# Conformer convolution: tap diagonals on ScalarE in place of GpSimd, lasting padded buffers, the last bias on VectorE

## The chip, the cores and the metric

The kernel runs on one core of a Trainium2 chip. The metric is device time in microseconds (us) of one execution, compared by the median of several runs. The engines are TensorE (PE in the profile: matmuls, with weight loads as PEld), VectorE (DVE), ScalarE (ACT) and GpSimd (POOL); SyncE (SP) issues the DMAs.

## The reference, cut to what matters

Eight residual stages run over 256 tokens of 1024 channels: a state-space and gated linear attention mixer, a feed-forward stage, latent attention, a feed-forward stage, retention with pooling, a feed-forward stage, the conformer convolution, a feed-forward stage. Only the seventh is touched:

```python
def conformer_conv(h, w_pw1, b_pw1, w_dw, b_dw, ln_g, ln_b, w_pw2, b_pw2):
    a, gate = jnp.split(h @ w_pw1 + b_pw1, 2, axis=-1)
    u = a * jax.nn.sigmoid(gate)
    dw = lax.conv_general_dilated(
        u, w_dw[:, None, :], window_strides=(1,), padding=((CONV_WIDTH_2 - 1, 0),),
        dimension_numbers=('NWC', 'WIO', 'NWC'), feature_group_count=D_MODEL) + b_dw
    ...
    z = (d32 - mu) * lax.rsqrt(var + EPS) * ln_g + ln_b
    z = jax.nn.silu(z).astype(h.dtype)
    return z @ w_pw2 + b_pw2
```

The depthwise convolution has 31 taps over time for each of 1024 channels, padded with 30 zeros on the left. The result, with the bias `b_pw2`, is added to the residual x.

## The kernel before

Every float32 product is made in three passes over two halves of each operand. The high half is a ScalarE copy, the low half a VectorE subtraction: for weights `hi` (L151) and `lo` (L152), pieces of 128x512; for activations in `split` (L156, L157). The three matmuls of a product are L283 to L285 (tokens on the output's partitions) or L289 to L291 (channels on them).

The conformer holds channels on partitions, eight channel tiles k of 128 channels. The string `ORDER = "p0 c01 p1 c23 s0 p2 c45 s1 p3 c67 s2 s3"` gives the order in which its steps are written:

- `p0` to `p3`: projection i makes channel tiles 2i and 2i+1. For each there are 48 matmuls of 128x256 into a bank `acc` (p0 has tokens on the partitions, is copied out as `rt`, L1081, and turned), then `sg` = sigmoid (ScalarE, L1096), `u` = gated product (VectorE, L1099), and its halves `uh` (ScalarE) and `ul` (VectorE), 128x286 with the margin of 30 zeros, which a GpSimd memset writes (L1098).
- `c01` to `c67`: the convolution of two channel tiles. `PE_TAPS = [13]*6 + [16, 18]`, 112 in all, says how many of a tile's 31 taps run on TensorE, as matmuls with diagonal matrices into a bank `pw`: three matmuls and two diagonals (high, low) for each tap. `diags` (L1038) makes up to eight taps' diagonals with one GpSimd instruction (L1044), in four rotating buffers `diag`. The other 136 taps are VectorE instructions over `u` that add into `d` (8 at L1141, 128 at L1143); then one instruction per tile adds the bank `pw` to `d` (L1146, the d add below).
- `s0` to `s3`: statistics of d. After `s3`, layer norm, silu (ScalarE, L1186) and the output projection, which adds to x.

The bias bp is added to x by two GpSimd instructions of 128x1024 (L1065) at the stage's start. A scheduler places instructions on each engine's queue by dependencies and priorities (`high_priority`, `issue_after`); each engine then runs its queue in order.

Of the kernel before, what the change touches and what calls it, by code (L numbers as in the profile page):

```python
# [17 lines left out]
P = 128  # L18
# [12 lines left out]
# how far a stage's splits of the weights may go ahead, and in how many steps  # L31
TUNE = [(150, 4), (1, 4), (400, 4), (1, 4), (1, 4), (1, 4), (400, 4), (1, 4)]
FIRST = 800  # priority of the chains that the tensor engine waits for
ORDER = "p0 c01 p1 c23 s0 p2 c45 s1 p3 c67 s2 s3"  # conformer: projections, convolutions, statistics
MORDER = "s0 p0 s1 v0 p1 n1 v1 s2 s3 v2 v3"  # attention: scores, second half of the projections, its norms, values
# [7 lines left out]
def T(t):  # L43
    return slice(t * P, (t + 1) * P)


def bc_row(v, n):
    """a DRAM vector of n values, the same for each partition"""
    return v.rearrange("(o c) -> o c", o=1).to_broadcast([P, n])


def cols(v):
    """a DRAM vector of 128*k values -> [128, k], value k*128+p on partition p"""
    return v.rearrange("(k p) -> p k", p=P)


class Net:
# [32 lines left out]
    def constants_later(self):  # L90
        nc, c, a = self.nc, self.cst, self.a
        g = nc.gpsimd
        self.identb = c.tile([P, P], BF16, name="identb")
        g.tensor_copy(self.identb, self.ident)
        self.tri = c.tile([P, P], F32, name="tri")
        g.affine_select(self.tri, self.ones, pattern=[[1, P]], base=0, channel_multiplier=-1, compare_op=ALU.is_ge, fill=0.0)
        zer = self.tmp.tile([P, 512], F32, tag="sq512", name="zer", bufs=1)
        g.memset(zer, 0.0)
        # SSD: [s, (chunk, l)], masked where l < s
        self.mneg_s = c.tile([P, 2, P], BF16, name="mneg_s")  # L100
        g.affine_select(self.mneg_s, zer[:, :256].rearrange("p (a b) -> p a b", a=2), pattern=[[0, 2], [1, P]], base=0, channel_multiplier=-1, compare_op=ALU.is_ge, fill=NEG)
        # attention: [q, k] masked where k > q
        self.mneg_a = c.tile([P, P], BF16, name="mneg_a")
        g.affine_select(self.mneg_a, zer[:, :P], pattern=[[-1, P]], base=0, channel_multiplier=1, compare_op=ALU.is_ge, fill=NEG)
        # one-hot rows: a head's high part lies in row h, its low part in row 32 + h
        self.sel = c.tile([P, 16], F32R, name="sel")
        self.nc.vector.tensor_add(self.sel, self.ident[:, 0:16], self.ident[:, 32:48])
# [6 lines left out]
    def columns(self, srcs, name, t=None, eng=None):  # L114
        """rows of 128 values in DRAM -> columns, in tiles of up to 128 of them; the second step is returned"""
        nc = self.nc
        n = sum(s.shape[0] for s in srcs)
        assert n <= P
        raw = self.tmp.tile([P, P], F32, tag="raw_col", name="raw_col", bufs=3)
        o = 0  # L120
        for s in srcs:
            (eng or nc.gpsimd).dma_start(out=raw[o:o + s.shape[0], :], in_=s)
            o += s.shape[0]
        if t is None:
            t = self.cst.tile([P, n], F32, name=name)

        def turn():
            b = self.bank("ptr", (P, P))
            nc.tensor.transpose(b[:, :n], raw[:n, :], self.ident[:n, :n])
            nc.vector.tensor_copy(t, b[:, :n])  # L130
        return t, turn

# [27 lines left out]
    def small_weights(self, W):  # L160
        """the columns of dt (0:16) and of the gate's low rank part (32:48)"""
# [9 lines left out]
    def load_x(self, x, g):  # L171
        """-> the first stage's gain on all partitions, in two banks"""
# [34 lines left out]
    def rsqrt_wide(self, v, n, pool):  # L207
        """v [P, n] -> 1 / sqrt(v) in place: a first value from the exponent's bits, three Newton steps"""
# [12 lines left out]
    def transposes(self, src, hi, lo, ncols):  # L221
        """src [128 tokens, ncols] -> hi/lo [128, ncols/128, 128]"""
# [8 lines left out]
    def transposes_f32(self, srcs, dst, rows=P, scale=None, eng="act"):  # L231
        """srcs [128, rows] each -> dst [rows, len, 128]"""
# [60 lines left out]
    def projA(self, w, evac, n=512, tok=(0, 1)):  # L293
        """w [1024, n<=512]: evac(t, bank [128 tokens, n])"""
# [10 lines left out]
    def projW(self, w, evac):  # L305
        """w [1024, 256]: evac(j, psum [128 columns, 256 tokens]) for its two column tiles"""
# [9 lines left out]
    def outproj(self, w, lhs, ks, after, tail=2, ahead=None, pieces=None):  # L316
        """x[t] += lhs^T @ w; after(t) is called when x[t] is whole. ks: order of the k tiles"""
# [72 lines left out]
    def mixer0(self, after):  # L390
# [3 lines left out]
        with self.stage("mix") as sp, self.stage("mixs") as ss:  # L394
# [34 lines left out]
            # ---- gates: log sigmoid, sums within the chunks of 64  # L429
# [14 lines left out]
            # ---- dt = softplus(x) = max(x, 0) + log1p(exp(-|x|)), log1p(e) = 2 atanh(e / (2 + e))  # L444
# [27 lines left out]
            # ---- the gates' sums and their exponentials  # L472
# [10 lines left out]
            # ---- x, B, C: projection, causal convolution, silu  # L483
# [20 lines left out]
            # exponents' parts on partitions: -acum of each chunk, and what is left of chunk 0  # L504
# [16 lines left out]
            # decay0[s, h, l] for s in chunk 0 and all l, decay1 for s and l in chunk 1  # L521
# [23 lines left out]
            # ---- the state-space part, y[p, l] for two heads at a time  # L545
# [8 lines left out]
            # ---- GLA values  # L554
# [3 lines left out]
            # ---- keys and queries with their decays  # L558
# [23 lines left out]
            # ---- GLA. Scores within a token tile: from an even chunk to the odd one the decay of the even chunk comes in  # L582
# [83 lines left out]
    def mla(self, after):  # L666
# [3 lines left out]
        with self.stage("mla") as sp, self.stage("mlap") as pp:  # L670
# [6 lines left out]
            with self.tc.issue_after(self.last_norm):  # L677
# [9 lines left out]
                # the norms' gains over the nope part, both for q  # L687
# [4 lines left out]
            # the low rank projections  # L692
# [5 lines left out]
            for t in range(2):  # L698
# [6 lines left out]
                with self.tc.high_priority(offset=FIRST):  # L705
# [12 lines left out]
                    if t == 1:  # L718
                        # the softmax's table, while the engine is free
                        nc.scalar.activation(ssq[:, 0:1], ssq[:, 0:1], AF.Exp)  # L720
                    nc.vector.tensor_scalar(kr[t].rearrange("p o j -> p (o j)"), c[:, QR + KR:672], r[:, 2:3], None, op0=ALU.mult)
            # rotation with the gains in it: out = x * rc + swap(x) * rs
# [13 lines left out]
            def rope(x, t, i, n):  # L736
                """x [P, n, 32] in SBUF, in place"""
# [11 lines left out]
            # q, k, v by heads, eight at a time  # L749
# [41 lines left out]
            def norms(i):  # L791
# [6 lines left out]
                # q's rope part takes the ratio of its two norms, the rest comes in with the softmax's scale  # L798
# [15 lines left out]
            # attention, four heads at a time  # L814
# [71 lines left out]
    def rotations(self, sp):  # L886
        """sines and cosines of positions * inv_freq: the angle is reduced in two steps with an exact three part 2 pi"""
# [29 lines left out]
        # cos = sin(pi/2 - |r|)  # L917
# [8 lines left out]
    def retention(self, after):  # L926
        nc, a = self.nc, self.a
        W = a["ret_w_in_2"][0]
        with self.stage("ret") as sp, self.stage("retp") as pp:
# [43 lines left out]
            # retention: keys of chunk 0 meet all queries, keys of chunk 1 the queries of theirs  # L973
# [39 lines left out]
            # pooling: sums over windows by doubling  # L1013
# [24 lines left out]
    def diags(self, pool, taps, k):  # L1038
        """the two halves of some taps' weights on diagonals: [128, (tap, half), 128]"""
        n = 2 * len(taps)  # L1040
        t = pool.tile([P, 16, P], F32R, tag="diag", name="diag", bufs=4)
        w = self.whl_dw[:, taps[0] % 2, taps[0] // 2:taps[0] // 2 + len(taps), :, k].rearrange("p a b -> p (a b)")
        w = w.rearrange("p (a o) -> p a o", o=1).to_broadcast([P, n, P])
        self.nc.gpsimd.affine_select(t[:, :n], w, pattern=[[0, n], [1, P]], base=0, channel_multiplier=-1, compare_op=ALU.is_equal, fill=0.0)  # L1044
        return t

    def conformer(self, after):
# [3 lines left out]
        with self.stage("conf") as sp, self.stage("confp") as pp:  # L1051
# [4 lines left out]
            # even taps, then odd ones  # L1056
# [4 lines left out]
            with self.tc.issue_after(self.last_norm):  # L1061
                bp = pp.tile([P, D], F32, name="bp")
                nc.sync.dma_start(out=bp, in_=bc_row(a["conv_b_pw2_2"][0], D))
                for t in range(2):
                    nc.gpsimd.tensor_add(self.x[t], self.x[t], bp)  # L1065
# [3 lines left out]
            def proj(i):  # L1069
                cs = slice(i * 256, i * 256 + 256)  # L1070
                ag = [self.load([W[:, cs]], 8, 256), self.load([W[:, D + i * 256:D + (i + 1) * 256]], 8, 256)]
                if i == 0:
                    # tokens on partitions, so that the first half can start before the second is normed; turned afterwards
# [9 lines left out]
                for j in range(2):  # L1083
# [10 lines left out]
                    with self.tc.high_priority(offset=FIRST):  # L1094
                        sg = sp.tile([P, 256], F32, tag="sg", name="sg", bufs=2)
                        nc.scalar.activation(sg, ps[:, 1, :], AF.Sigmoid, bias=self.bp1[:, 8 + k:9 + k])  # L1096
                        u = sp.tile([P, H + S], F32, tag="u", name="u", bufs=4)
                        nc.gpsimd.memset(u[:, :H], 0.0)  # L1098
# [4 lines left out]
                        if k == 7:  # L1103
                            # the table of the norm's silu, while the engine is free
# [3 lines left out]
            def conv(ks):  # L1108
                """some taps on the tensor engine, the others on the vector engine"""
                bs, rest = {}, {}  # L1110
                for k in ks:
# [5 lines left out]
                    if n_odd:  # L1117
                        # float32r operands start on 8 bytes: a copy that is one ahead for the odd taps
# [45 lines left out]
            # layer norm over the channels: statistics with tokens on the partitions, then mean and deviation along the tokens  # L1164
# [14 lines left out]
            for w in (1, 1, 2, 2, 2):  # L1179
# [8 lines left out]
                k += w  # L1188
            self.outproj(a["conv_w_pw2_2"][0], lambda k, t: (zTh[:, k, T(t)], zTl[:, k, T(t)]), list(range(8)), after, ahead=1)
# [99 lines left out]
```

## Time and profile before

| | us |
|---|---|
| median of 3 runs | 1350.18 |
| lowest, highest | 1350.11, 1351.87 |
| span of the profiled execution | 1351.1 |

The profiled execution has no time beside its span. The span lies within the three runs, so nothing measurable lies around it, and it is 0.9 us above their median. TensorE's mean granted clock is 0.986 of full speed. The conformer's convolutions take 1009.3 to 1119.0 us of the span. The profile is read from the page's totals to the windows of that stretch, then to the waits in it, and to single instructions on the timelines.

### The profile page before, as it was taken

How to read it: one execution, taken by the hardware profiler on the slowest of the kernel's cores; microseconds unless marked ns; L12 is line 12 of the kernel's file. 1: busy time of each engine (PE TensorE's matmuls, PEld its weight loads, DVE VectorE, ACT ScalarE, POOL GpSimd, SP SyncE). 2: the span in 40 equal slices, each digit the busy share in tenths (PEclk: the TensorE clock that was granted, in tenths of full speed). 3: DMA queues.
4: the chain of work that ended last, by engine and by line, in shares of the span. 5: the costliest groups of instructions: out<-in, count | busy, mean ns of one | idle time of the engine just before them, and what ended most of it. 6: DMA issues, size and time to landing. Idle time of an engine off the chain costs nothing.

```text
span 1351.1 us, 21552 instructions
## 1 busy us (share of the span) xinstructions
PE 1289.8 (95%) x8562; PEld 1174.5 (87%) x8562; DVE 874.6 (65%) x1720; ACT 661.4 (49%) x1410; POOL 97.9 (7%) x111
## 2 busy tenths in 40 slices
PE   5999999999999999999999999999999797999997
PEld 4979888999988867999987889999879796999986
DVE  4868565655545887755547777555469997655544
ACT  3783454545544876554444535554443223544542
POOL 3000000000000000000000000000016440000000
PEclk9999999999999999999999999999999897999999
DMA  6546344655554423655655544555653104455551
GB/s 186 168 156 203 116 156 165 203 182 178 179 208 133 162 95 107 226 179 179 213 191 172 184 159 166 177 181 180 217 171 110 68 28 134 164 186 187 187 199 50
DMA packets 152495, 219.75 MB, mean 163 GB/s; under 512 B 8371, under 2 KB 121499, under 8 KB 152396
## 3 DMA queue, kind: packets, MB, share of 16 engines
q1 hardware_dynamic: 151018, 214.04, 47.4%
q0 software_dynamic: 1376, 4.34, 0.9%
q8 instruction: 67, 1.10, 0.3%
q14 instruction: 32, 0.26, 0.1%
q10 hardware_dynamic: 2, 0.00, 0.0%
HBM read 217.33 MB, written 1.05 MB: 162 GB/s over the span
## 4 chain that ended last, share of the span: by engine, by line
PE 81%; DVE 10%; ACT 3%; issue 3%; DMA 1%; POOL 1%; SPq 0%; POOLq 0%; DVEq 0%; ACTq 0%
PE acc L290 11%; PE acc L291 11%; PE acc L289 11%; PE acc L329 8%; PE acc L330 8%; PE acc L333 8%; PE acc L285 4%; PE acc L283 4%; PE acc L284 4%; DVE lo L152 3%; PE pw L289 3%; PE pw L290 3%; PE pw L291 3%; DVE d L1143 2%; PE ptr L228 1%
## 5 line engine op out<-in xcount | busy, mean ns | idle before, releaser
L152 DVE TENSOR_TENSOR lo<-raw,hi 128x512 fp32r<-128x512 f32 (+2 forms) x800 | 515.0, 689 | 239.3 <-ACT hi L151 238.0
L151 ACT CAST hi<-raw 128x512 fp32r<-128x512 f32 (+2 forms) x800 | 444.8, 616 | 312.0 <-PE acc L333 104.2
L291 PE MATMUL acc<-xTh,lo 128*128 128x256 f32 x1312 | 372.7, 284 | 0.7 <-DVE lo L152 0.7
L289 PE MATMUL acc<-xTh,hi 128*128 128x256 f32 x1312 | 373.3, 285 | 0.0
L290 PE MATMUL acc<-xTl,hi 128*128 128x256 f32 x1312 | 372.9, 284 | 0.0
L291 PEld LDWEIGHTS acc<-xTh,lo 128*128 128x128 f32 x1312 | 253.0, 193 | 0.9 <-DVE lo L152 0.9
L290 PEld LDWEIGHTS acc<-xTl,hi 128*128 128x128 f32 x1312 | 253.1, 193 | 0.2
L289 PEld LDWEIGHTS acc<-xTh,hi 128*128 128x128 f32 x1312 | 253.0, 193 | 0.2
L330 PE MATMUL acc<-lo,hTh 128*128 128x512 f32 x352 | 137.3, 390 | 0.0
L329 PE MATMUL acc<-hi,hTh 128*128 128x512 f32 x352 | 137.3, 390 | 0.0
L283 PE MATMUL acc<-hi,xTh 128*128 128x512 f32 (+2 forms) x352 | 120.2, 341 | 0.0
L285 PE MATMUL acc<-hi,xTl 128*128 128x512 f32 (+2 forms) x352 | 119.3, 339 | 0.5 <-DVE xTl L157 0.5
L284 PE MATMUL acc<-lo,xTh 128*128 128x512 f32 (+2 forms) x352 | 119.6, 340 | 0.0
L333 PE MATMUL acc<-hi,hTl 128*128 128x512 f32 x352 | 113.5, 389 | 0.0
L204 POOL TENSOR_TENSOR r<-v,nhalf 128x1 f32<-128x1 f32 (+1 forms) x24 | 16.3, 679 | 993.6 <-DVE v L265 937.3
L289 PE MATMUL pw<-xTh,hi 128*128 128x256 f32 x264 | 76.1, 288 | 8.4 <-ACT xTh L156 8.4
L382 DVE TENSOR_TENSOR h<-sg,acc 128x256 f32<-128x256 f32 x72 | 30.0, 417 | 80.0 <-ACT sg L381 79.8
L381 ACT ACTIVATE sg<-acc 128x256 f32<-128x256 f32 x72 | 27.6, 383 | 104.8 <-PE acc L291 98.8
L333 PEld LDWEIGHTS acc<-hi,hTl 128*128 128x128 f32 x352 | 66.1, 188 | 13.6
L329 PEld LDWEIGHTS acc<-hi,hTh 128*128 128x128 f32 x352 | 66.1, 188 | 13.6
L330 PEld LDWEIGHTS acc<-lo,hTh 128*128 128x128 f32 x352 | 66.1, 188 | 13.4
L290 PE MATMUL pw<-xTl,hi 128*128 128x256 f32 x264 | 76.1, 288 | 0.0
(399 smaller groups left out, 1889.9 us busy)
## 6 DMA issues: line engine op xcount, KB each, us to landing
raw<-w_in_even SPq DMA_DIRECT2D x22, 1024.0 KB, 5.1
raw<-w_gate SPq DMA_DIRECT2D x22, 1024.0 KB, 5.3
raw<-w_up SPq DMA_DIRECT2D x22, 1024.0 KB, 5.3
raw<-w_down SPq DMA_DIRECT2D x22, 1024.0 KB, 4.8
raw<-ffn_w_gate SPq DMA_DIRECT2D x22, 1024.0 KB, 5.2
raw<-ffn_w_up SPq DMA_DIRECT2D x22, 1024.0 KB, 5.1
raw<-ffn_w_down SPq DMA_DIRECT2D x22, 1024.0 KB, 4.8
raw<-conv_w_pw SPq DMA_DIRECT2D x12, 1024.0 KB, 5.2
```

What stands on the lines that cost most here:

```text
L151: nc.scalar.copy(fl(hi)[:, c], fl(raw)[:, c])
L152: nc.vector.tensor_sub(fl(lo)[:, c], fl(raw)[:, c], f32(fl(hi)[:, c]))
L283: mm(out, lh, wh, start=first, stop=False)
L284: mm(out, lh, wl, start=False, stop=False)
L285: mm(out, ll, wh, start=False, stop=last)
L289: mm(out, wh, xh, start=first, stop=False)
L290: mm(out, wh, xl, start=False, stop=False)
L291: mm(out, wl, xh, start=False, stop=last)
L329: nc.tensor.matmul(b, lh, hi[:, j, cs], start=st, stop=False)
L330: nc.tensor.matmul(b, lh, lo[:, j, cs], start=False, stop=False)
L333: nc.tensor.matmul(banks[t][h], ll, hi[:, j, cs], start=False, stop=sp)
L382: nc.vector.tensor_mul(h, sg, ps[:, 1, :])
```

## The change

`diags` fills the same four rotating buffers, but by 224 ScalarE instructions of 128x128, each a copy of the identity scaled by one column of `whl_dw` (a scale that is read from memory, one value per partition). The GpSimd instruction is gone. The tiles `u` are four lasting buffers, whose margins are cleared once at the stage's start (four memsets instead of eight). The bias is added to x on VectorE, and stands in the code just ahead of the output projection. In other functions comments alone are removed.

```diff
     def diags(self, pool, taps, k):
-        n = 2 * len(taps)
         t = pool.tile([P, 16, P], F32R, tag="diag", name="diag", bufs=4)
-        w = self.whl_dw[:, taps[0] % 2, taps[0] // 2:taps[0] // 2 + len(taps), :, k].rearrange("p a b -> p (a b)")
-        w = w.rearrange("p (a o) -> p a o", o=1).to_broadcast([P, n, P])
-        self.nc.gpsimd.affine_select(t[:, :n], w, pattern=[[0, n], [1, P]], base=0, channel_multiplier=-1, compare_op=ALU.is_equal, fill=0.0)
+        for n, tap in enumerate(taps):
+            for half in range(2):
+                w = f32(self.whl_dw[:, tap % 2, tap // 2, half, k:k + 1])
+                self.nc.scalar.activation(t[:, 2 * n + half, :], self.ident, AF.Copy, scale=w)
         return t
...
                 nc.sync.dma_start(out=bp, in_=bc_row(a["conv_b_pw2_2"][0], D))
-                for t in range(2):
-                    nc.gpsimd.tensor_add(self.x[t], self.x[t], bp)
+
+                ubuf = [sp.tile([P, H + S], F32, name=f"u{i}") for i in range(4)]
+                for u in ubuf:
+                    nc.gpsimd.memset(u[:, :H], 0.0)
...
-                        u = sp.tile([P, H + S], F32, tag="u", name="u", bufs=4)
-                        nc.gpsimd.memset(u[:, :H], 0.0)
+                        u = ubuf[k % 4]
...
+            for t in range(2):
+                nc.vector.tensor_add(self.x[t], self.x[t], bp)
             self.outproj(a["conv_w_pw2_2"][0], lambda k, t: (zTh[:, k, T(t)], zTl[:, k, T(t)]), list(range(8)), after, ahead=1)
```

The scheduler also moves instructions that the diff doesn't name. The rows below are instructions in queue order: line, operation, output and inputs, the output's shape, and a count where a row repeats.

On VectorE, at the end of `p0`, from the split of the convolution's weights (`whl_dw`) to the first low halves `ul`, the queue of before is:

```order
L157 TENSOR_TENSOR whl_dw<-wdw,whl_dw 128x15x8
L152 TENSOR_TENSOR lo<-raw,hi 128x512 x8
L1099 SCALAR_TENSOR_TENSOR u<-acc,lp,sg 128x256 x2
L1141 TENSOR_SCALAR d<-u,wdw,lp 128x256
L157 TENSOR_TENSOR ul<-u,uh 128x286 x2
```

and the queue of the change at the same place is:

```order
L157 TENSOR_TENSOR whl_dw<-wdw,whl_dw 128x15x8
L1191 TENSOR_TENSOR x_82<-x_82,bp 128x1024
L1191 TENSOR_TENSOR x_83<-x_83,bp 128x1024
L152 TENSOR_TENSOR lo<-raw,hi 128x512 x5
L1100 SCALAR_TENSOR_TENSOR u_10214<-acc,lp,sg 128x256
L1100 SCALAR_TENSOR_TENSOR u_10215<-acc,lp,sg 128x256
L152 TENSOR_TENSOR lo<-raw,hi 128x512
L157 TENSOR_TENSOR ul<-u_10214,uh 128x286
L157 TENSOR_TENSOR ul<-u_10215,uh 128x286
L152 TENSOR_TENSOR lo<-raw,hi 128x512 x2
```

The two bias adds (L1191) stand ahead of the first u, although the code has them at the stage's end, and three of the eight `lo` have moved behind the first u.

On ScalarE, at the same place, from the second copy out of p0's banks to the gate of the third channel tile, the queue of the change is:

```order
L1083 COPY rt<-acc 128x512
L151 CAST hi<-raw 128x512
L1098 ACT_TABLE_LOAD
L1098 ACTIVATE sg<-acc,lp 128x256 x2
L151 CAST hi<-raw 128x512
L156 CAST uh<-u_10214 128x286
L156 CAST uh<-u_10215 128x286
L151 CAST hi<-raw 128x512 x2
L1044 ACTIVATE diag<-ident,whl_dw 128x128 x36
L1098 ACTIVATE sg<-acc,lp 128x256
L1044 ACTIVATE diag<-ident,whl_dw 128x128 x4
L156 CAST uh<-u_10216 128x286
```

Before, all eight `hi` stood ahead of that copy, the two `uh` were followed at once by the third gate, and no diagonal stood in the queue. Now 36 diagonals stand between the first `uh` and that gate; the first 18 of the 224 stand ahead of these rows.

At the end of the convolutions, from the copies for the odd taps of the last tile to the first silu (L1187), ScalarE's queue of the change is:

```order
L1122 CAST uh_11400<-uh 128x285
L1123 CAST ul_11401<-ul 128x285
L1044 ACTIVATE diag<-ident,whl_dw 128x128 x36
L151 CAST hi<-raw 128x512 x12
L1187 ACTIVATE d<-d,lp 128x256
L156 CAST zTh<-d 128x256
```

Before, one `hi` stood between those copies and the first silu; now 36 diagonals and 12 `hi` do.

## Rows read from the trace of the kernel before

**Rows 1.** The page: busy time of each engine, and GpSimd's row of 40 slices.

```profile
PE 1289.8 (95%) x8562; PEld 1174.5 (87%) x8562; DVE 874.6 (65%) x1720; ACT 661.4 (49%) x1410; POOL 97.9 (7%) x111
...
POOL 3000000000000000000000000000016440000000
```

**Rows 2.** Windows: stretch, length, busy time (instructions) by engine, clock, DMA share, GB/s.

```profile
1009.30:1119.00 109.70, 93.54 (x718) 91.90 (x717) 102.82 (x194) 30.24 (x59) 58.07 (x24) 0.92 0.22 73
486.00:488.00 2.00, 1.08 (x5) 0.80 (x6) 2.00 (x8) 2.00 (x9) 0.00 (x0) 1.00 0.00 0
1042.00:1046.00 4.00, 4.00 (x35) 4.00 (x35) 4.00 (x4) 2.61 (x5) 4.00 (x3) 1.00 0.00 0
1055.00:1060.00 5.00, 4.97 (x24) 5.00 (x25) 5.00 (x12) 0.00 (x0) 0.00 (x0) 0.52 0.46 179
```

**Rows 3.** Waits, 1009.2 to 1119.4: total us, times, longest us.

```profile
ACT sg L1096 <- PE acc L291: 40.9, 3, 15.8
POOL diag L1044 <- PE pw L291: 25.4, 4, 8.4
...
PE pw L289 <- DVE d L1146: 9.4, 3, 4.1
```

**Rows 4.** VectorE's timeline: start us, length us, instructions, [idle before them, releaser].

```profile
1000.97 1.42 DVE L269 SCALAR_TENSOR_TENSOR xn<-x,r,gain 128x512 f32<-128x512 f32 x2 [0.75 <-POOL r L204]
...
1006.87 1.28 DVE L152 TENSOR_TENSOR lo<-raw,hi 128x512 fp32r<-128x512 f32 x2
...
1009.27 3.49 DVE L269 SCALAR_TENSOR_TENSOR xn<-x,r,gain 128x512 f32<-128x512 f32 x2 [0.44 <-POOL r L204]
1012.69 3.93 DVE L152 TENSOR_TENSOR lo<-raw,hi 128x512 fp32r<-128x512 f32 x2
...
1020.90 8.82 DVE L152 TENSOR_TENSOR lo<-raw,hi 128x512 fp32r<-128x512 f32 x8 [2.09 <-ACT hi L151]
...
1031.80 9.58 DVE L1143 SCALAR_TENSOR_TENSOR d<-u,wdw,d 128x256 f32<-128x256 f32 x24
1041.52 0.48 DVE L1099 SCALAR_TENSOR_TENSOR u<-acc,lp,sg 128x256 f32<-128x256 f32 x1
...
1070.11 0.48 DVE L1099 SCALAR_TENSOR_TENSOR u<-acc,lp,sg 128x256 f32<-128x256 f32 x1 [1.95 <-ACT sg L1096]
...
1097.32 0.48 DVE L1099 SCALAR_TENSOR_TENSOR u<-acc,lp,sg 128x256 f32<-128x256 f32 x1 [2.71 <-ACT sg L1096]
...
1118.68 0.74 DVE L1146 TENSOR_TENSOR d<-d,pw 128x256 f32<-128x256 f32 x2
```

**Rows 5.** GpSimd's timeline, same columns.

```profile
1009.22 2.33 POOL L1065 TENSOR_TENSOR x<-x,bp 128x1024 f32<-128x1024 f32 x1
...
1034.61 13.73 POOL L1044 TENSOR_SCALAR_AFFINE_SELECT diag<-whl_dw 128x2048 fp32r<-128x2048 f32 x4 [8.44 <-PE pw L291]
```

**Rows 6.** VectorE's instruction groups by form, 1009.2 to 1119.4: busy us, mean ns, idle.

```profile
L1143 DVE SCALAR_TENSOR_TENSOR d<-u,wdw,d 128x256 f32<-128x256 f32 x128 | 59.8, 533 | 0.0
...
L157 DVE TENSOR_TENSOR ul<-u,uh 128x286 fp32r<-128x286 f32 x8 | 8.2, 1035 | 0.0
```

**Rows 7.** ScalarE's timeline in the first mixer, columns as above.

```profile
86.12 0.36 ACT L529 ACTIVATE dec<-pw,bi 128x128 f32<-128x128 f32 x1
...
88.93 0.38 ACT L531 ACTIVATE dec<-pw,bi 128x128 f32<-128x128 f32 x1
```

**Rows 8.** ScalarE's instruction groups by form, whole span.

```profile
L156 ACT CAST hTh<-h 128x256 fp32r<-128x256 f32 x80 | 32.5, 406 | 19.5 <-DVE h L382 19.5
...
L156 ACT CAST hTh<-ptr 128x256 fp32r<-128x256 f32 x8 | 3.0, 372 | 6.2 <-PE ptr L228 6.2
```

**Rows 9.** ScalarE's timeline in the conformer.

```profile
1023.08 2.18 ACT L151 CAST hi<-raw 128x512 fp32r<-128x512 f32 x4 [0.65 <-PE acc L285]
...
1025.77 1.28 ACT L1096 ACT_TABLE_LOAD   x1
...
1127.60 0.60 ACT L1186 ACTIVATE d<-d,lp 128x256 f32<-128x256 f32 x1 [16.54 <-DVE d L1184]
```

## The prediction

> **What bounds the kernel now.** I read the page first: TensorE is busy for 95% of the span, GpSimd for 7%, and GpSimd's slices show nearly all of that in the first slice and in four late ones [rows 1]. The late ones are the conformer's convolutions. There the first window is read: of 109.7 us TensorE is busy 93.5, VectorE 102.8, GpSimd 58.1, and ScalarE only 30.2 [rows 2]. So VectorE, not TensorE, is nearly full there, and ScalarE has room. The waits of the stretch agree: ScalarE's gates wait 40.9 us for TensorE in three stalls, TensorE in its turn waits 9.4 us for d adds, and GpSimd has 25.4 us of rests in which it waits for a free `diag` buffer [rows 3]. The last wait of the stage is therefore VectorE's taps, ending with the d add at 1118.68 [rows 4].
>
> Then I read why VectorE is full, by looking for the same instruction at two speeds. A pair of `xn` takes 1.42 us at 1000.97 and 3.49 us at 1009.27; two `lo` take 1.28 us at 1006.87 and 3.93 at 1012.69; eight take 8.82 us, 1.10 each, against 0.64 [rows 4]. The slow ones lie where GpSimd works: the first bias add runs 1009.22 to 1011.55 [rows 5]. The 128 taps average 533 ns, though 24 in a row take 9.58 us, 0.40 each [rows 4, 6]; the eight `ul` average 1035 ns, and are as large as a tap [rows 6]. The penalty is not even: those 24 taps end at 1041.38, while GpSimd has made selects since 1034.61, and the four selects beside them took 13.73 us [rows 4, 5]. In such a meeting sometimes the one engine is held up, sometimes the other.
>
> **What the change is worth.** It takes GpSimd's selects and bias adds away, so VectorE should run at its undisturbed speeds, and it gives ScalarE 224 instructions. I work forward from one u to the next, taking at each the engine that is last.
>
> *The price of a diagonal.* The trace has no ScalarE copy of 128x128 with a scale from memory. The nearest are 12 instructions of 128x128 with a bias from memory, which start at 86.12 to 88.93: 2.81/11 = 0.255 us apart, each lasting 0.36 to 0.38 [rows 7]. They read PSUM; a diagonal reads SBUF, and the same cast of 128x256 takes 406 ns from SBUF against 372 from PSUM, +0.034 [rows 8]. I take 0.255 + 0.034 = 0.29 us. Bounds: 0.25 (the rows' pace as it is) and 0.38 (no overlap of one with the next). All 224 cost 65 us at 0.29; ScalarE had 109.7 − 30.2 = 79.5 us idle [rows 2], so the stage fits, but only just, and the two engines become equals.
>
> The Trainium skill, "ScalarE: Activation LUTs", section "What ACT_TABLE_LOAD costs", speaks against moving such work there: 186 ns plus 0.833 ns per element, 93 ns more for each operand that is a pointer, 93 ns given back where instructions follow each other. By that a diagonal is estimated at 293 ns overlapped and 386 ns not, so 224 of them at 66 or 86 us; the sum below would stand by the first, and by the second lose 0.096 × 206 = 19.8 us, all of its gain. The rows above show the overlap.
>
> *Start of the stage.* With no bias add on GpSimd, `xn` costs 3.49 − 1.42 = 2.07 less and the `lo` pair 3.93 − 1.28 = 2.65 less: 4.7 us, of which I take 4.0 for the end of p0, since TensorE's turning of xn lies between. The bias adds cost VectorE about 2 × 1.12 = 2.2 us (a 128x512 `lo` at 0.64, plus 512 columns more at (0.64 − 0.40)/256 = 0.94 ns, by the difference of `lo` and tap). They stand ahead of the first u, not late as the change says. But VectorE now idles 2.09 us there for the next `hi` [rows 4]: they fill that, and I cost them at nothing; without that cover, 2.2.
>
> *First u.* Before, eight `lo`, 8.82 us from 1020.90, end where the first u begins, at 1029.64. After, three of them stand behind u. p0's last matmuls end at 1023.08, where the four `hi` that wait for them start [rows 9]; 4.0 sooner is 1019.1. Behind that ScalarE does a copy (about 0.6, as 128x512 `hi` do), one `hi` of 0.55 (2.18/4), a table load of 1.28 [rows 9] and a gate of about 0.45: 2.9 us, first u at 1022.0, **7.6 us sooner**.
>
> *Third u (1041.52).* VectorE has 25 taps at 0.40, three `lo` at 0.64, two u and two first taps at 0.35 to 0.4 and two `ul` at 0.37 (a tap's size): 14.0 us. ScalarE has 36 diagonals (10.4), three `hi`, two `uh` and a gate: about 13.4. Third u at 1036.0, **5.5 sooner**; 2.1 of the gain goes back to the moved `lo`.
>
> *Fifth u (1070.11).* The cycle before took 28.6 us. After, VectorE has 34 taps (13.6), eight `lo` (5.1), two u, two `ul`, two d adds and two first taps (2.9): 21.6. ScalarE has 53 diagonals (15.4), eight `hi` (4.4) and 1.4 for gates and `uh`: 21.2. TensorE has 78 + 96 matmuls at 0.12 (4.00 us for 35, clock 1.00 [rows 2]): 20.9. Fifth u at 1057.6, **12.5 sooner**.
>
> *Seventh u (1097.32).* The cycle took 27.2. VectorE has 21.4 by the same count, ScalarE 61 diagonals, four `hi` and the 1.4, 21.3: **18.3 sooner**.
>
> *Second d add of the last pair (1118.68).* It came 21.4 us after the seventh u. Now ScalarE is last: 56 diagonals (16.2), one table load (1.28), and gate, `uh` and the odd taps' copies (2.4) make 19.9, so **19.8 sooner**. The 12 `hi` behind the last diagonals (6.5 us) must end before the first silu, but that starts at 1127.60 [rows 9], 8.6 us after the d adds end at 1119.0: hidden with 2.1 us to spare. Each u also needs a handoff between engines whose queues are now both full; I give back about 0.45 us for each of four, 1.8 in all (a choice; it could be nothing): **−18.0 us**.
>
> What lies behind the stage is the same work in the same order, so it moves as a whole. The four memsets that fall away ran beside other work and are put at nothing, as the lasting buffers are. The profiled execution took 1351.1 us, within the runs shown and 0.9 above their median. 1351.1 − 18.0 = 1333.1: I predict **1333 us**.
>
> **The rivals.** *Diagonals without overlap (B).* 206 diagonals follow the first `uh`. Every 0.01 us over 0.29 costs 2.06 us, since ScalarE then sets every cycle; at 0.38 that is 18.5 us, the whole gain: 1339 to 1351. For it: each reads its scale from a different address, and no row shows that operand. Against it: the rows that take a different bias each keep 0.255.
>
> *VectorE isn't freed (C).* If the slow rows are due to something else than GpSimd, only VectorE's idle time comes back: 2.1, 1.95 and 2.7 us at 1020.90, 1070.11 and 1097.32 [rows 4], and ScalarE's load eats some of it: about 1346 to 1351. Against it: the slow `xn` begin 0.05 us after a bias add [rows 4, 5], and the same pair 8 us earlier is fast.
>
> The Trainium skill, "SBUF — State Buffer", section "SBUF: two separate sides", has VectorE operations with two SBUF inputs and GpSimd operations that read SBUF share a port pair as an exclusive lock. The slow `xn` beside the bias add agrees; by the 24 taps at 0.40 beside slow selects it is GpSimd that loses there.
>
> *A slow TensorE (D), the other side.* Each tap's three matmuls come when two diagonals are ready, 0.58 us apart, and hold TensorE for 0.36. If its clock then falls to the lower level of 1.2 GHz, a matmul takes 5.00/24 = 0.208 (clock 0.52) in place of 0.12 [rows 2]. All 336 convolution matmuls at that pace cost 336 × 0.088 = 29.6 us more, up to 1363; slower than before from 18/0.088 = 205 of them on. For it: in 1055 to 1060 the clock was at half after TensorE had stood 4 us waiting for a d add [rows 2, 3]. Against it: in 486 to 488 TensorE was busy 1.08 of 2.00 us at clock 1.00 [rows 2].
>
> **Chances and range.** My forecast 0.74 (1327 to 1339: from diagonals at 0.25, where VectorE is the bound, to 0.32), B 0.15, C 0.04, D 0.07. The range runs from 1326 to 1344, and leaves out half of B, C and D, 0.18. What this kernel's measurement can tell from no change is about 0.2%, 2.7 us. Faster by more than that: 0.74, 0.11 of B, 0.02 of C: 0.87. Within: 0.03 of B, 0.02 of C: 0.05. Slower: D and 0.01 of B: 0.08.
>
> **What would show it.** In the profile after: `xn` and `lo` at 1.4 and 1.3 us a pair at the stage's start; 128 taps at a mean near 0.40 us, `ul` near 0.37; `diag` groups on ScalarE with a pace of 0.29; u of the third, fifth and seventh tile some 14, 21.6 and 21.4 us apart; the two bias adds in what was VectorE's idle time ahead of the first u; GpSimd nearly idle. I am wrong if the diagonals' pace passes 0.33, if taps stay near 0.53, if the clock falls to half for most of the convolutions, or if the first silu waits for `hi` and not for the norm.

## The result, and the profile after

The change takes 1328.12 us (median of 4 runs, 1327.98 to 1328.32) against 1350.14 for the kernel before in the same session: ratio 0.9838, 95% interval 0.9826 to 0.985, 22.0 us less. The forecast was 1333, with a range of 1326 to 1344.

In the page of the changed kernel (each engine's busy time, GpSimd's slices) GpSimd has left the stretch, and ScalarE is 64 us busier, what 224 diagonals were priced at:

```profile
PE 1280.7 (97%) x8562; PEld 1166.1 (88%) x8562; DVE 855.5 (65%) x1722; ACT 725.7 (55%) x1634; POOL 40.9 (3%) x88
...
POOL 3100000000000000000000000000000000000000
```

The window of the same stretch, from the norm's `xn` to the second d add of the last pair (columns as in [rows 2]):

```profile
1006.75:1096.40 89.65, 88.64 (x721) 87.11 (x719) 84.09 (x198) 89.14 (x274) 0.78 (x5) 1.00 0.28 89
```

109.7 us have become 89.65. TensorE was busy for 93.5 of 109.7 at a mean clock of 0.92 [rows 2]; now for 88.6 of 89.65 at 1.00. ScalarE is as full (89.1), VectorE nearly so (84.1). The last wait has changed hands: from the first u (1019.40) to 1092.94 none of the three rests for more than 0.1 us at a time, and the longest wait left is VectorE's for the last bank, 3.00 us.

VectorE's timeline of the changed kernel, with the rows that answer to [rows 4]:

```profile
998.44 1.41 DVE L269 SCALAR_TENSOR_TENSOR xn<-x,r,gain 128x512 f32<-128x512 f32 x2 [0.75 <-POOL r L204]
...
1006.75 1.41 DVE L269 SCALAR_TENSOR_TENSOR xn<-x,r,gain 128x512 f32<-128x512 f32 x2 [0.44 <-POOL r L204]
1008.08 1.29 DVE L152 TENSOR_TENSOR lo<-raw,hi 128x512 fp32r<-128x512 f32 x2
...
1011.48 2.35 DVE L1191 TENSOR_TENSOR x<-x,bp 128x1024 f32<-128x1024 f32 x2
1014.17 2.50 DVE L152 TENSOR_TENSOR lo<-raw,hi 128x512 fp32r<-128x512 f32 x4 [0.35 <-ACT hi L151]
...
1019.40 0.88 DVE L1100 SCALAR_TENSOR_TENSOR u<-acc,lp,sg 128x256 f32<-128x256 f32 x2 [1.10 <-ACT sg L1098]
...
1033.38 0.47 DVE L1100 SCALAR_TENSOR_TENSOR u<-acc,lp,sg 128x256 f32<-128x256 f32 x1
...
1054.49 0.47 DVE L1100 SCALAR_TENSOR_TENSOR u<-acc,lp,sg 128x256 f32<-128x256 f32 x1
...
1075.87 0.48 DVE L1100 SCALAR_TENSOR_TENSOR u<-acc,lp,sg 128x256 f32<-128x256 f32 x1
...
1095.94 0.42 DVE L1147 TENSOR_TENSOR d<-d,pw 128x256 f32<-128x256 f32 x1 [3.00 <-PE pw L291]
```

The two profiled executions are not level when the stage begins: `xn` starts at 1006.75 here and at 1009.27 before, a difference of 2.5 us that has arisen in the first mixer, long before the first changed instruction. So places are compared from each kernel's own `xn` at the stage's start (us):

| place | before | after | change | forecast |
|---|---|---|---|---|
| first u | 20.37 | 12.65 | −7.7 | −7.6 |
| third u | 32.25 | 26.63 | −5.6 | −5.5 |
| fifth u | 60.84 | 47.74 | −13.1 | −12.5 |
| seventh u | 88.05 | 69.12 | −18.9 | −18.3 |
| end of the last d add (1119.42; 1096.36) | 110.15 | 89.61 | −20.5 | −19.8 |
| first silu (1127.60; 1103.87) | 118.33 | 97.12 | −21.2 | |
| end of the span | 341.83 | 319.55 | −22.3 | |

The instruction groups of VectorE in the changed kernel's stage (busy us, mean ns):

```profile
L1144 DVE SCALAR_TENSOR_TENSOR d<-u,wdw,d 128x256 f32<-128x256 f32 x128 | 52.3, 475 | 0.1
L152 DVE TENSOR_TENSOR lo<-raw,hi 128x512 fp32r<-128x512 f32 x24 | 15.4, 683 | 1.3 <-ACT hi L151 1.3
L1100 DVE SCALAR_TENSOR_TENSOR u<-acc,lp,sg 128x256 f32<-128x256 f32 x8 | 3.7, 476 | 1.2 <-ACT sg L1098 1.1
L157 DVE TENSOR_TENSOR ul<-u,uh 128x286 fp32r<-128x286 f32 x8 | 3.5, 449 | 0.0
...
L1142 DVE TENSOR_SCALAR d<-u,wdw,lp 128x256 f32<-128x256 f32 x8 | 3.0, 403 | 0.0
```

Taps have gone from 533 to 475 ns and `ul` from 1035 to 449 [rows 6]. A mean here is a length: each tap begins before the one ahead of it has ended, so taps of 475 ns follow each other every 0.40 us. The busy time counts such an overlap once: 59.8 us [rows 6] have become 52.3.

ScalarE's timeline of the changed kernel, two long runs of diagonals, the copies behind the last of them, and the first silu:

```profile
1021.84 10.66 ACT L1044 ACTIVATE diag<-ident,whl_dw 128x128 fp32r<-128x128 f32 x36
...
1084.81 10.66 ACT L1044 ACTIVATE diag<-ident,whl_dw 128x128 fp32r<-128x128 f32 x36
1095.37 6.32 ACT L151 CAST hi<-raw 128x512 fp32r<-128x512 f32 x12
1103.87 0.60 ACT L1187 ACTIVATE d<-d,lp 128x256 f32<-128x256 f32 x1 [2.18 <-DVE d L1185]
```

One diagonal lasts 0.39 us (median of the 224), so the pace is (10.66 − 0.39)/35 = 0.293 us.

### The profile page after: what moved, and what is told of

It is laid out like the page before. It is cut to its first block, busy times and chain, and to the rows that moved or that the text cites. A ratio compares the mean times of both kernels' runs of the same rounds, so it can differ in the third digit from the quotient of the medians.

```text
span 1326.3 us, 21722 instructions
## 1 busy us (share of the span) xinstructions
PE 1280.7 (97%) x8562; PEld 1166.1 (88%) x8562; DVE 855.5 (65%) x1722; ACT 725.7 (55%) x1634; POOL 40.9 (3%) x88
## 4 chain that ended last, share of the span: by engine, by line
PE 86%; DVE 6%; ACT 3%; issue 2%; DMA 1%; POOL 1%; SPq 0%; POOLq 0%; DVEq 0%; ACTq 0%
PE acc L290 12%; PE acc L289 12%; PE acc L291 12%; PE acc L329 8%; PE acc L330 8%; PE acc L333 8%; PE acc L285 4%; PE acc L283 4%; PE acc L284 4%; PE pw L289 4%; PE pw L291 3%; PE pw L290 3%; DVE lo L152 2%; PE ptr L228 2%; DMA raw<-w_in_even 1%
## 5 line engine op out<-in xcount | busy, mean ns | idle before, releaser
L152 DVE TENSOR_TENSOR lo<-raw,hi 128x512 fp32r<-128x512 f32 (+2 forms) x800 | 508.9, 682 | 236.1 <-ACT hi L151 234.9
L291 PE MATMUL pw<-xTh,lo 128*128 128x256 f32 x264 | 75.8, 287 | 0.0
```

What stands on the lines that cost most here:

```text
L152: nc.vector.tensor_sub(fl(lo)[:, c], fl(raw)[:, c], f32(fl(hi)[:, c]))
L291: mm(out, wl, xh, start=False, stop=last)
```

## The experiments

My theory: GpSimd's selects and bias adds held VectorE up, and nothing else in the change matters; afterwards ScalarE, VectorE and TensorE are equally full. The rivals: the gain comes from the new order of the queues; ScalarE alone is the new bound; the lasting tiles or the place of the adds have a part in it.

| run | us, median | ratio to before, 95% interval |
|---|---|---|
| the change | 1328.12 | 0.9838, 0.9826 to 0.985 |
| e1, diagonals alone | 1333.51 | 0.9882, 0.9868 to 0.9897 |
| e2, bias adds alone | 1347.94 | 0.9986, 0.9977 to 0.9996 |
| e3, lasting u alone | 1350.36 | 1.0003, 0.9993 to 1.0012 |
| e4, dummy selects | 1354.61 | 1.0032, 1.0021 to 1.0044 |
| e5, dummy memsets | 1343.78 | 0.9955, 0.994 to 0.997 |
| e6, constant scale (other values than the reference's) | 1326.73 | 0.9823, 0.9807 to 0.984 |
| e7, 16 taps | 1326.60 | 0.9827, 0.9813 to 0.9842 |
| e8, bias late | 1330.76 | 0.9854, 0.9839 to 0.9868 |
| e9, half the memsets | 1329.26 | 0.9841, 0.9826 to 0.9856 |
| e10, 15 taps | 1328.90 | 0.9836, 0.9819 to 0.9852 |

**e1, the diagonals alone.** Of the change only this is kept:

```diff
-        self.nc.gpsimd.affine_select(t[:, :n], w, pattern=[[0, n], [1, P]], base=0, channel_multiplier=-1, compare_op=ALU.is_equal, fill=0.0)
+                self.nc.scalar.activation(t[:, 2 * n + half, :], self.ident, AF.Copy, scale=w)
```

> The diagonals alone go to ScalarE; the bias adds stay on GpSimd and the u tiles rotate with eight memsets, as before. My theory (GpSimd's selects and bias adds held VectorE up): everything of the change comes but the start of the stage, where xn and the first lo pair stay slow: 4.0 to 4.7 us less gain than the change's 22, about 1332 us (1330.5 to 1334). Rival: the gain has little to do with GpSimd and comes from the new order of the queues: then the bias adds' place is worth nothing and this runs at 1328.

As the theory has it: 1333.5. VectorE's timeline in e1, then GpSimd's:

```profile
1006.90 3.50 DVE L269 SCALAR_TENSOR_TENSOR xn<-x,r,gain 128x512 f32<-128x512 f32 x2 [0.44 <-POOL r L204]
1010.32 3.96 DVE L152 TENSOR_TENSOR lo<-raw,hi 128x512 fp32r<-128x512 f32 x2
...
1023.94 0.88 DVE L1099 SCALAR_TENSOR_TENSOR u<-acc,lp,sg 128x256 f32<-128x256 f32 x2 [1.09 <-ACT sg L1096]
```

```profile
1006.84 2.34 POOL L1065 TENSOR_TENSOR x<-x,bp 128x1024 f32<-128x1024 f32 x1
...
1011.31 2.40 POOL L1065 TENSOR_TENSOR x<-x,bp 128x1024 f32<-128x1024 f32 x1
```

Each bias add lies on one slow pair, as before, and the first u comes 17.0 us after `xn` (12.65 in the change). All later `lo` and taps run undisturbed.

**e2, the bias adds alone** (`nc.gpsimd.tensor_add` out, `nc.vector.tensor_add` ahead of the output projection in).

> The two bias adds alone move to VectorE (the scheduler puts them ahead of the first u here too); GpSimd still makes the diagonals. My theory: xn and the first lo pair fall to 1.4 and 1.3 us, so p0 ends 4 us sooner, but the 2.35 us of bias adds now lie on a VectorE that the selects still slow down: 1346 to 1348. Rival: 0, 1350, since the time comes back in the selects' contention.

1347.9: 2.2 us of the 4.7 are left. VectorE's timeline in e2 shows where the rest went: `xn` is fast, but the selects start earlier too, and the eight `lo` beside them take 10.29 us (8.82 before [rows 4]).

```profile
1006.35 1.41 DVE L269 SCALAR_TENSOR_TENSOR xn<-x,r,gain 128x512 f32<-128x512 f32 x2 [0.44 <-POOL r L204]
...
1013.82 10.29 DVE L152 TENSOR_TENSOR lo<-raw,hi 128x512 fp32r<-128x512 f32 x8 [0.38 <-ACT hi L151]
```

So the parts don't add up: 16.6 and 2.2 apart, 22.0 together. The missing 3 us are little more than the scatter of the three runs taken together; from `xn` to the end of the span the traces have 16.9 and 3.1 of 22.3. The adds' place is worth 5.4 once the selects are gone (e1 against the change; the lasting tiles, which differ too, give nothing by e3).

**e3, the lasting u tiles alone** (`u = ubuf[k % 4]`, four memsets at the stage's start).

> The lasting u tiles with four memsets alone. My theory: nothing, 1349 to 1351. Rival: the weight loads of the convolution that the profile of before shows waiting 7.5 us for the memsets of u really wait for them: 2 to 7 us faster.

No difference: the 7.5 us of weight loads waiting, which the list of waits put down to those memsets, are not won back. In e3's trace the loads still wait 10.6 us, with no cause in the list (before, 4.1 without a cause and the 7.5); so those memsets were not what held them.

**e4, dummy selects beside the change.**

```diff
+        m = n // 2
+        for i in range(2):
+            extra = pool.tile([P, 8, P], F32R, tag="extra", name="extra", bufs=1)
+            w = uh[:, i * m:i * m + m].rearrange("p (a o) -> p a o", o=1).to_broadcast([P, m, P])
+            self.nc.gpsimd.affine_select(extra[:, :m], w, pattern=[[0, m], [1, P]], base=0, channel_multiplier=-1, compare_op=ALU.is_equal, fill=0.0)
```

> The changed kernel, with GpSimd making as many selects as before (in halves), into a tile that nobody reads, from the start of uh; the output is the same. My theory: VectorE loses again what the selects cost it before, some 12 to 17 us on lo, ul and the taps (they measured 930, 1035 and 533 ns before, 683, 449 and 475 now): 1340 to 1346. Rival (VectorE is not held up by GpSimd, the order of the queues made the gain): 1328, all three means as in the changed kernel.

1354.6: the order of the queues alone gains nothing. The scheduler moved a few VectorE instructions here (two first taps stand ahead of four `lo` that they follow in the change), but e9 below has nearly the same queue and runs at 1329.3. The direction is the theory's, the size is not: 26 us are lost, more than the change had gained. VectorE's groups in e4:

```profile
L1150 DVE SCALAR_TENSOR_TENSOR d<-u,wdw,d 128x256 f32<-128x256 f32 x128 | 70.3, 615 | 0.1
L152 DVE TENSOR_TENSOR lo<-raw,hi 128x512 fp32r<-128x512 f32 x25 | 18.7, 797 | 0.3 <-ACT hi L151 0.3
L157 DVE TENSOR_TENSOR ul<-u,uh 128x286 fp32r<-128x286 f32 x8 | 4.4, 563 | 0.0
```

Taps lose 70.3 − 52.3 = 18 us, more than the 7.5 of before. The selects wait for `uh` here, so they all begin just behind a u, where taps run. In the kernel before, three batches began inside a run of taps, and their first selects took 8.65, 9.67 and 9.62 us, each ending 1.9 us behind that run, against 1.3 to 2.2 for the others of these batches: there GpSimd waited, and the taps kept their pace. GpSimd's timeline of before, the first of the four selects in [rows 5]:

```profile
1034.61 8.65 POOL L1044 TENSOR_SCALAR_AFFINE_SELECT diag<-whl_dw 128x2048 fp32r<-128x2048 f32 x1 [8.44 <-PE pw L291]
```

One place behind a u in GpSimd's timeline of e4 and in VectorE's:

```profile
1040.57 4.46 POOL L1050 TENSOR_SCALAR_AFFINE_SELECT extra<-uh 128x1024 fp32r<-128x1024 f32 x4 [8.85 <-ACT uh L156]
```

```profile
1040.99 4.31 DVE L1150 SCALAR_TENSOR_TENSOR d<-u,wdw,d 128x256 f32<-128x256 f32 x4
```

Four selects and four taps in the same 4.4 us: each tap stands for one select, 1.08 us in place of 0.40. In all VectorE is busy 21.8 us longer (105.9 against 84.1). The other 4.5 us are waits: those for gates take 7.0 us against 1.1 in the change. They lie behind TensorE: the window from `xn` to the last d add shows it at a mean clock of 0.88, and its longest waits are for d adds again.

```profile
1007.47:1123.40 115.93, 96.77 (x721) 94.47 (x719) 105.89 (x198) 93.46 (x282) 37.77 (x39) 0.88 0.21 69
```

**e5 and e9, dummy memsets.** What e5's expectation takes from the Trainium skill stands in "SBUF — State Buffer", section "SBUF: two separate sides".

```diff
+        m = n // 2
+        for i in range(2):
+            extra = pool.tile([P, 8, P], F32, tag="extra", name="extra", bufs=1)
+            self.nc.gpsimd.tensor_copy(extra[:, 0, 0:1], f32(uh[:, 0:1]))
+            for _ in range(2):
+                self.nc.gpsimd.memset(extra[:, :m], 0.0)
```

> The same with GpSimd memsets in place of the selects, two for each half select, each set behind a copy of one column of uh: GpSimd writes SBUF as much or more, and reads next to nothing. If only a GpSimd instruction that reads SBUF holds VectorE up, as a page of the Trainium skill has it: 1328 to 1329. Rival (any busy GpSimd does): 5 us or more over 1328, lo and ul slow as in e4.

1343.8, which by the number is the rival's. By the rows it is not: taps 477 ns, `lo` 682, `ul` 448. Nearly all the time is lost at one place, in GpSimd's and VectorE's timelines of e5:

```profile
1115.16 0.68 POOL L1051 MEMSET extra<- 128x256 f32 x2
1115.81 0.72 POOL L1181 TENSOR_TENSOR lnr<-rm,nhalf 128x2 f32<-128x2 f32 x1
```

```profile
1116.57 0.16 DVE L1182 SCALAR_TENSOR_TENSOR rm<-mv,lnr 128x2 f32<-128x2 f32 x1 [13.85 <-POOL lnr L1181]
```

The norm's one GpSimd instruction stood behind the dummies. e9 has one memset where e5 has two.

> As e5 with half the memsets. There taps, lo and ul kept the undisturbed 477, 682 and 448 ns, and the 15.7 us came from the norm's instruction on GpSimd, which stood behind the last memsets and kept VectorE waiting 13.85 us. My theory: GpSimd's writes don't hold VectorE up; with its queue empty by the end of the convolutions this runs at 1328 to 1330. Rival (the writes cost something by themselves): about half of e5's loss, 1335 or more.

1329.3, and taps of 474 ns: GpSimd's writes don't hold these instructions up. e9 shows more of the mechanism. VectorE's groups and timeline, then GpSimd's timeline:

```profile
L1150 DVE SCALAR_TENSOR_TENSOR d<-u,wdw,d 128x256 f32<-128x256 f32 x128 | 52.5, 474 | 0.1
...
L1148 DVE TENSOR_SCALAR d<-u,wdw,lp 128x256 f32<-128x256 f32 x8 | 4.5, 590 | 0.0
```

```profile
1085.46 9.19 DVE L1150 SCALAR_TENSOR_TENSOR d<-u,wdw,d 128x256 f32<-128x256 f32 x23
```

```profile
1086.66 0.51 POOL L1049 COPY extra<-uh 128x1 f32<-128x1 f32 x1
1087.22 0.95 POOL L1050 MEMSET extra<- 128x1024 f32 x1
1088.24 6.46 POOL L1049 COPY extra<-uh 128x1 f32<-128x1 f32 x1
1094.76 0.95 POOL L1050 MEMSET extra<- 128x1024 f32 x1
1095.78 0.18 POOL L1049 COPY extra<-uh 128x1 f32<-128x1 f32 x1
```

A GpSimd copy of one column takes 0.18 us where VectorE lets it, and 6.46 where it stands beside a run of 23 taps: it ends at 1094.70, as that run does (1094.65). The copy before it began in the same run and got in after 0.51. Four copies in e9 were held to the end of a run of taps (5.18, 6.05, 8.03 and 6.46 us), while others that began early in such runs took 0.20 to 0.51; what decides between them no run here shows. So a run of two-input VectorE instructions without a gap can keep GpSimd out to its end, and a GpSimd instruction that reads SBUF, once in, keeps VectorE out (e4). The first taps (one tensor input, 403 ns in the change) are slower even beside memsets, 590 ns, 1.5 us for the eight. By the same section of the Trainium skill VectorE instructions with two SBUF inputs share an exclusive lock with GpSimd instructions that read SBUF, and those in a faster two-port mode with any GpSimd instruction. For two inputs the traces of e4 and e9 agree (taps of 615 and 474 ns); that the first taps run in such a mode no run here shows.

**e6, a constant scale.**

```diff
-                self.nc.scalar.activation(t[:, 2 * n + half, :], self.ident, AF.Copy, scale=w)
+                self.nc.scalar.activation(t[:, 2 * n + half, :], self.ident, AF.Copy, scale=0.5)
```

> The changed kernel with a constant 0.5 as the scale of each diagonal in place of the tap's weight, so the taps' values on TensorE are not the reference's. It prices the scale that is read from memory: the pace should fall from 0.295 to about 0.20 us. My theory: ScalarE, VectorE and TensorE are equals in the cycles, so only the tail after the seventh u (36 diagonals, VectorE idle 3.0 us for the bank) gains: 1 to 4 us, 1324 to 1327. Rival (ScalarE alone sets the stage): 206 x 0.09 = 18 us, 1310.

1326.7, 1.4 us below the change; the intervals overlap, and by the traces the last d add ends 87.51 us after `xn` (89.61). ScalarE's timeline of e6, then its window of the stage:

```profile
1021.85 10.72 ACT L1044 ACTIVATE diag<-ident 128x128 fp32r<-128x128 f32 x53
...
1044.25 9.92 ACT L1044 ACTIVATE diag<-ident 128x128 fp32r<-128x128 f32 x49 [0.96 <-PE pw L291]
```

```profile
1007.00:1094.00 87.00, 86.41 (x719) 85.62 (x717) 84.45 (x198) 73.49 (x283) 0.57 (x1) 1.00 0.28 91
```

The pace falls to (10.72 − 0.30)/52 = 0.200 us, and ScalarE now waits for TensorE to leave a `diag` buffer. TensorE stays full, 86.4 of 87.0 us, VectorE again rests for no more than 0.2 us at a time between the first u and the last bank, and the seventh u comes 69.18 us after `xn` (69.12): cheaper diagonals have nothing to give here beyond the tail.

**e7 and e10, fewer taps of the last tile on TensorE** (18 in the change).

```diff
-PE_TAPS = [13] * 6 + [16, 18]
+PE_TAPS = [13] * 6 + [16, 16]
```

> The changed kernel with 16 of the last channel tile's taps on TensorE in place of 18: four diagonals and the two copies for odd taps leave ScalarE (2.0 us) ahead of the last bank, two taps (0.8 us) go to VectorE, which idles 3.0 us there. My theory (ScalarE sets the tail): 1.5 to 2 us faster than the changed kernel, about 1326.3. Rival (the tail is covered by the norm's chain or by TensorE): 1328.

1326.6, and by the traces, which tell more than the overlapping intervals, the last d add ends 87.75 us after `xn` (89.61): VectorE's wait for the last bank falls from 3.00 us to 0.38. This is the fastest of the versions run that compute the reference. VectorE's timeline of e7:

```profile
1094.72 0.42 DVE L1147 TENSOR_TENSOR d<-d,pw 128x256 f32<-128x256 f32 x1 [0.38 <-PE pw L291]
```

e10 writes 15 in place of that 16.

> As e7 with 15 of the last tile's taps on TensorE in place of 16: ScalarE loses two more diagonals (0.59 us), TensorE three matmuls (0.36), VectorE gets a tap (0.40), and idled 0.38 us for the last bank in e7. My theory: within 0.5 us of e7, 1326.2 to 1327; rival (ScalarE still sets the end): 0.6 us or more below it.

Neither: 1328.9, some 2 us above e7. VectorE's timeline of e10 shows why:

```profile
1094.86 0.68 DVE L152 TENSOR_TENSOR lo<-raw,hi 128x512 fp32r<-128x512 f32 x1
1095.46 0.47 DVE L1144 SCALAR_TENSOR_TENSOR d<-u,wdw,d 128x256 f32<-128x256 f32 x1
1095.85 0.68 DVE L152 TENSOR_TENSOR lo<-raw,hi 128x512 fp32r<-128x512 f32 x1
1096.46 0.41 DVE L1147 TENSOR_TENSOR d<-d,pw 128x256 f32<-128x256 f32 x1
```

With one more tap the scheduler has put two `lo` ahead of the last d add, 1.2 us of work that nobody waits for at that moment. The other 0.8 us lie behind that d add, and I did not follow them up.

**e8, the bias adds late.** `with self.tc.issue_after(self.last_d):` around the two adds, where `last_d` is the last d add.

> The changed kernel with the two bias adds held back behind the last d add on VectorE, so they really come late, among the statistics of the norm. My theory: their early place costs nothing, since ScalarE sets the first u and TensorE never waits in the stage, so moving them gains nothing; in the norm's chain 1.2 us of them stand ahead of the first silu, which TensorE waits for: 1328 to 1330. Rival (early adds delay the first u by their 2.35 us): 1326.

1330.8, a little above my range: late adds cost 2.2 us by the ratios, whose intervals overlap. They stand in the norm's chain, where TensorE's wait for the norm's GpSimd result grows from 3.5 to 4.6 us. The first u comes 12.66 us after `xn`, as in the change (12.65), so the early adds delay nothing.

## Why the prediction was right, point by point

The mechanism was right in each step, and five places of the table fall within 0.8 us of their forecast. The forecast itself was 5 us too high, all of it by terms that are named at the end.

**VectorE freed** (rival C out): shown from both sides, by e1's slow pair beside each bias add and by e4, which brings the selects back, with e9 as its control. One reading was loose: the prediction set the taps' mean length, 533 ns, beside their pace, 0.40 us, and forecast a mean near 0.40. The length to compare with is 475, so the selects cost the taps 7.5 us, less than those two numbers suggest. The sum counted taps at their pace and was not touched.

**The start of the stage.** p0's last matmul ended 13.8 us after `xn` and now ends 9.6 after it, 4.2 sooner. The 4.0 of the sum was a choice, not worked out, and it came out.

**The price of a diagonal**, 0.29: 0.293 (rival B out). The twelve rows it was taken from last 0.35 to 0.39 us, not 0.36 to 0.38; the sum used their pace alone. The operand from memory, which no row of before had, costs 0.293 − 0.200 = 0.093 by e6, and one diagonal overlaps the next by 0.39 − 0.293 = 0.097. By the Trainium skill, "ScalarE: Activation LUTs", section "What ACT_TABLE_LOAD costs", which the prediction weighed, a diagonal is estimated at 293 ns overlapped, 93 of them for the pointer. These rows agree.

**The bias adds** took 2.35 us (2.2 forecast) in VectorE's wait for `hi`, as said, and cost nothing there (e8).

**The cycles** were forecast at 14.0, 21.6 and 21.4 us and measured 13.98, 21.11 and 21.38. In them VectorE hardly rests (0.1 us at most), as the sum had it. The 12 `hi` behind the last diagonals were hidden too: the first silu waits another 2.18 us for the norm's d (2.1 forecast).

**A slow TensorE** (rival D out): its clock was 1.00 throughout the stage. In the cycles it had `acc` matmuls beside the `pw` ones and ran at its full pace. At the end, where the diagonals alone feed it, the window shows 47 matmuls in 7.00 us, against 35 in 4.00 [rows 2], and the clock still at 1.00:

```profile
1088.00:1095.00 7.00, 7.00 (x47) 6.22 (x45) 4.94 (x13) 7.00 (x25) 0.00 (x0) 1.00 0.01 2
```

**What was mis-sized.** The step is "I give back about 0.45 us for each of four, 1.8 in all", for handoffs. There were none: the last d add came 20.5 us sooner, not 18.0. Of the 0.7 beyond the 19.8 of the sum without handoffs, 0.5 lie in the fifth tile's cycle. I read it so: an engine that is late by less than the work the next one has in stock makes nobody wait, and each had taps, matmuls or diagonals in stock; no run tests this. The second step is "it moves as a whole": 1.7 us more came behind the stage. Of these 0.7 lie before the first silu; half of the last statistics' instructions now run while VectorE waits for the last bank, 3.00 us. The other 1.1 lie behind it, where the output projection's stretch of low clock is shorter; the windows of 22.0 us before and 20.9 after, up to the next stage's norm, are these:

```profile
1128.00:1150.00 22.00, 21.31 (x81) 17.23 (x82) 14.87 (x27) 12.26 (x25) 0.00 (x0) 0.84 0.52 169
```

```profile
1104.30:1125.20 20.90, 20.24 (x81) 16.54 (x82) 16.04 (x29) 12.24 (x25) 0.03 (x1) 0.90 0.47 148
```

Both hold 81 matmuls; the mean clock is 0.84 and 0.90. Why the clock came back sooner I did not test. 20.5 + 0.7 + 1.1 = 22.3, the medians' 22.0. The third step is the base, 1351.1: a span was taken for a time, on the ground that nothing lies around the span. The changed kernel's profiled execution has a span of 1326.3 and a time of 1327.98. In e1's session the kernel before took 1350.17 with a span of 1348.3, and 1353.08 with one of 1351.2; so the profiled execution of before was a long one, some 3 us above the median, most of it the 2.5 us of the first mixer. A sum from the median of 1350.14 would have come out 1.0 us lower.

## What to carry to other kernels

Look for the same instruction at two speeds: where VectorE's pace changes with what GpSimd does, GpSimd's work is not free, however idle its row looks, and can cost VectorE as much time as it takes itself (4.7 us beside two bias adds of 4.7 [rows 4]). Work that moves to an engine with room is priced from that engine's pace, not from an instruction's length, and one sums up what every engine has per cycle: here three became about equally full, and none of the cheaper parts tried afterwards gave more than 2 us. Parts of a change on one contended resource don't add: measured alone, each leaves the contention to the other.

## What was not expected of the hardware

A GpSimd instruction that reads a single column of SBUF can take 6.46 us in place of 0.18, ending with a run of two-input VectorE instructions without a gap (e9); in the same run a memset of 128x1024 keeps its 0.95 us. And TensorE's mean clock in this stage went with its stalls: 0.92 in the kernel before, 0.88 with dummy selects, 1.00 in the change, where TensorE stood for 1.0 of 89.65 us.
